# The third pair of feed-forward blocks by seven quarter products, and five lesser weight parts by adding transfers

## The chip, the cores and the metric

The kernel runs on one core of a Trainium2 chip. The metric is the time of one execution on the device in microseconds. The kernel before was timed in three runs: median 947.94 us, lowest 947.19, highest 948.01. The profile is of one more execution, which took 947.17 us, with a span of 945.5 us from its first to its last instruction.

The engines are named as in the profile: PE is TensorE's matmuls and PEld its weight loads, DVE is VectorE, ACT ScalarE, POOL GpSimd, SP SyncE. A trailing q (SPq, POOLq) is the engine's sequencer, which issues transfers.

## The reference

One layer of a streaming encoder block over 512 tokens of 1024 numbers, in float32. The change touches only its first step, a feed-forward block of 2816 hidden numbers:

```python
def _swiglu(x, w_in, w_out):
    gate, up = jnp.split(x @ w_in, 2, axis=-1)
    return (jax.nn.silu(gate) * up) @ w_out

h = h + 0.5 * _swiglu(_rmsnorm(h, ffn1_norm[i]), ffn1_w_in[i], ffn1_w_out[i])
```

Here `w_in` is 1024 x 5632 (2816 columns of gate, 2816 of up) and `w_out` 2816 x 1024. Behind it stand the mixer (convolution and gated linear attention), a second feed-forward block, a gated input embedding and a last norm; they stay as they are.

## The kernel before

**Two parts of every number.** Matmuls run on float32r. A float32 weight is split in a larger part `wh`, its rounding to float32r, and a lesser part `wl`, what the rounding left; activations likewise (`hgH` and `hgL`, `t2H` and `t2L`, `actH` and `actL`). A product is three matmuls (`mm3`, L209, and `mul`, L308): wh with the larger activation, wh with the lesser, wl with the larger. `high` (L183) makes wh with a cast on ACT. The lesser part is made in one of two ways. `low` (L193) subtracts wh from the raw weights on DVE. `added` (L198) writes the negated rounding of the raw weights to wl with a second pass on ACT; then a transfer issued from POOL adds the raw weights onto it in place:

```python
act.mul(l3, r3, -1.0)
pool.dma_start(out=l3.bitcast(F32), in_=r3, accum_op=ALU.add)
```

In the first feed-forward block every lesser part is made by `low`; `added` is used in the mixer, in the second feed-forward block and at the end.

**Pairs.** The 22 blocks of 128 hidden numbers are taken in 11 pairs (0 to 10; the third pair is pair 2). A pair's input weights are four tiles of 128 x 1024 numbers (512 KB): a11, a12 (gate columns, first and second half of the 1024 inputs), a21, a22 (up columns). Activations are held turned, hidden numbers in partitions, tokens in columns. Pair 0 is computed in the opening, while x arrives.

A *plain* pair takes eight units h0 to h7 (`plain_unit`, L694), each 12 matmuls 512 columns wide. Any other pair is computed as a 2 x 2 matrix of blocks times a 2 x 2 matrix (two halves of the inputs by two halves of the tokens) with seven quarter products in place of eight: units m1, m2, m6, m7, m5, m4, m3 (L659 to L692), each 24 matmuls 256 wide. These need four sums of weight tiles, s1 = a21 + a22, s2 = s1 - a11, s3 = a11 - a21, s4 = a12 - s2 (`s12`, `s3_`, `s4_`, on DVE; s3 and s4 overwrite the raw tiles a21 and a12), each split in two parts, and sums of activations t1 to t4 (class `Right`, L329), which are made once and used by all such pairs. t4 overwrites the tiles of a part of the plain activations, so it is made after the last plain unit.

In the kernel before, pairs 1 and 2 are plain (`plain` is `(1, 2)`) and pairs 3 to 10 take seven products.

**Output blocks.** When the hidden numbers of a stretch of `CUTS` are finished (pairs 0 and 1 for the first), four output units follow; each multiplies one w_out tile of 512 KB and yields two blocks of the output, 12 matmuls 512 wide for each. They are put between the units of the pairs behind.

**Order.** `ffn` (L604) lists the units; `drive` (L584) walks through them. A unit names what it needs and how many units ahead: the load of a raw tile 7 or 9 units, the sums 6, the two parts of a tile `AHEAD` = 4 (5 for s1). The jobs due ahead of a unit are issued first, then the first gating job left by the unit before, then the unit's matmuls and its hook, then what else was left (`act_parts` splits the gated product in actH and actL). PE, DVE and ACT each execute their instructions strictly in this program order (class `Ordered`); POOL's and SP's instructions are ordered by the scheduler. So a job on ACT or DVE that is not ready holds all behind it on that engine.

Hooks hang other work on units: `first_out` with pair 0's gating on h0 of pair 1; the pieces and row sums for `Right` on h1, h2, h3 of pair 1 (tiles xg); and the splitting of t2, t3, t1, t4 on the units named at L869.

**Buffers.** Raw weight tiles have six (`raw`), wh and wl six each, weight sums two, PSUM banks for matmuls seven. The raw buffer of a tile comes free when its last reader is done: `low` on DVE, a sum, or with `added` the transfer. A load on SP's queue waits for its buffer and holds the loads behind it.

Of the kernel before, what the change touches and what calls it, by code (L numbers as in the profile page):

```python
# [62 lines left out]
def block_kernel(ctx: ExitStack, tc: tile.TileContext, a: dict, out: bass.AP):  # L63
# [29 lines left out]
    def tmp(s, w=SEQ, dt=F32, bufs=2):  # L93
        return tp.tile([P, w], dt, tag=s, bufs=bufs, name=nm(s))

    def bank():
        return pp.tile([P, SEQ], F32, tag="mm", bufs=7, name=nm("ps"))

    def aux():
        return pp.tile([P, SEQ], F32, tag="aux", bufs=1, name=nm("ax"))  # L100
# [158 lines left out]
    def spread(col, copy=True):  # L259

        ps = aux()
        for j in range(TB):
            pe.transpose(ps[:, j * P:(j + 1) * P], col[:, j:j + 1].to_broadcast([P, P]), ident)
        if not copy:
            return ps
        bc = tmp("bc", bufs=1)
        act.copy(bc, ps)
        return bc
# [255 lines left out]
    ps0 = [bank() for _ in range(4)]  # L524
    split_w(0, 1, dve.tensor_copy)
    split_x(0)
    mid = []
# [22 lines left out]
    xb = Right(hg, "ffn1_norm")  # L550
# [31 lines left out]
    AHEAD = 4  # L582
# [18 lines left out]
        for f in left:  # L601
            f()

    def ffn(w_in, w_out, x, gname, given, first, rsb, hooks, plain):  # L604


        norm = Norm()
# [86 lines left out]
        def plain_unit(j):  # L694

            up, i, k = j // 4, j // 2 % 2, j % 2
            def run(p):
                if not j:
                    p.g, p.s = {}, {}
                if not k:  # L700
                    p.x = bank()
                ps = p.x
                wh, wl = p.part(f"a{1 + up}{1 + k}")
                cs = slice(i * P, (i + 1) * P)
                for c in range(4):
                    mm3(ps, wh[:, c, cs], wl[:, c, cs], *x.rows[4 * k + c], k == c == 0, k == 1 and c == 3)
                if not k:
                    return []
                if not up:
                    def gate():  # L710
                        p.s[i] = silu(scaled(ps, "g1"))
                    return [gate]
                return [lambda: gated_block(p, p.s[i], scaled(ps, "u1"), i),
                        lambda: act_parts(p) if i else None]
            return run
# [4 lines left out]
        def unit(kind, i):  # L720
            p = pairs[i]

            def go(run):
                left = run(p)
                hooks.get((kind, i), lambda *_: None)()
                return left

            if kind[0] == "h":
                j = int(kind[1])
                part, run = (f"a{1 + j // 4}{1 + j % 2}", plain_unit(j)) if j % 4 < 2 else (None, plain_unit(j))  # L730
                if part:
                    return [(AHEAD, lambda: p.part(part)), (9, lambda: p.fetch(part))], lambda: go(run)
            else:
                part, run = USES[kind]
            before = [(AHEAD + (kind == 'm5'), lambda: p.part(part))] if part else []
            if kind in ("m1", "m2"):
                before.append((7, lambda: p.fetch(part)))
            elif kind == "m6":
                before += [(9, lambda: p.fetch("a21", "a22")), (6, p.s12)]
            elif kind in ("m7", "m3"):  # L740
                before.append((6, p.s3_ if kind == "m7" else p.s4_))

            return before, lambda: go(run)
# [63 lines left out]
        def add(kind, i):  # L807
            if 0 <= i < npair and (kind, i) not in had:
                had.add((kind, i))
                units.append(unit(kind, i))  # L810
# [48 lines left out]
    w_in = a["w_in"][0]  # L859
    w_ahead = []  # L860

    def sums_hooks(x, names, at):

        h = {}
        for name, key in zip(names, at):
            h[key] = lambda *_, name=name: x.split(name)
        return h

    hooks = sums_hooks(xb, ("t2", "t3", "t1", "t4"), (("h5", 1), ("h7", 1), ("h3", 2), ("m1", 3)))  # L869
    hooks.update({("h%d" % (i + 1), 1): f for i, f in enumerate(steps[2:])})  # L870
    hooks.update({("m5", 3): lambda *_: made[0](), ("m5", 4): lambda *_: constants(),
                  ("m4", 10): lambda *_: w_ahead.append(ahead(w_in, D_CONV, 2 * P)),
                  ("last", 4): lambda *_: w_ahead.append(ahead(w_in, 0, 2 * P))})
    hg, norm = ffn(ffn1_in, a["ffn1_w_out"][0], xb, "mix_norm", {0: Left(ffn1_in, 0), 1: w1},
                   (ps0[:2], ps0[2:]), lambda: spread(mid[0]), hooks, (1, 2))
    pool.on = False
    cw, gwu, mean, mask, nbias = made

# [61 lines left out]
    mid = []  # L940
# [10 lines left out]
    rs, rsb = mid  # L951
# [471 lines left out]
    mid = []  # L1423
    xb = Right(hg, "ffn2_norm")
# [15 lines left out]
    hooks = sums_hooks(xb, ("t2", "t3", "t1", "t4"), (("h0", 1), ("h1", 1), ("h3", 1), ("m1", 2)))  # L1440
# [3 lines left out]
    q11, q21, q12, q22, b11, b21, t2, wproj = ([] for _ in range(8))  # L1444
# [59 lines left out]
    def todo(*fs):  # L1504
# [6 lines left out]
                  ("rest", 4): todo((q_high, b21, q21, 1), (first_sum, 1), (third_sum, 1)),  # L1511
                  ("rest", 6): todo((final_in,), (row_sums, 0))})
    hg, norm = ffn(ffn2_in, a["ffn2_w_out"][0], xb, "ple_norm", wf, ((g0, u0), (g1_, u1_)), mid[1], hooks, (1,))


# [144 lines left out]
    def kept(ps, name, **kw):  # L1660
        o = tmp(name, **kw)
        act.copy(o, ps)
        return o
# [20 lines left out]
    t1, t3 = q11, q12  # L1684
    n2_ = [x for jp in range(2) for x in split_rows(n2, jp)]
    project(0)
    m1 = [kept(p_, "sq", bufs=3) for p_ in x_]
# [98 lines left out]
```

## Time and profile before

| | |
|---|---|
| median of three runs | 947.94 us |
| the profiled execution | 947.17 us |
| its span | 945.5 us |
| ACT busy | 471.6 us (50%) |
| POOL busy | 56.4 us (6%) |
| mean granted TensorE clock | 0.997 of full speed |
| DMA, mean over the span | 119 GB/s |

A timeline row gives the start and the length in us, the engine, the line of the code (all operations that go through the helper `Ordered` have its line, 46), the operation and its tiles (written from read). The length of one matmul holds its way through the array, which overlaps the next one's; what counts on a busy PE is the distance of two starts. In square brackets stands how long the engine had been idle and what ended it. A row for a stretch (A:B) gives its length, then for each engine the busy time and the number of instructions, then the clock, the DMA engines' busy share and GB/s. A row for transfers gives the tiles, the queue, the count, the size and, where the trace has it, the time from issue to landing.

### The profile page before, as it was taken

The page shows a single profiled execution, that of the slowest core. Times are in us where ns is not written, and L with a number is a line of the kernel's source. Part 1 is how long each engine was busy: PE and PEld are TensorE (multiplying, and loading weights), DVE is VectorE, ACT ScalarE, POOL GpSimd, SP SyncE. Part 2 cuts the span into 40 slices and gives each one's busy share as a digit, 9 for nine tenths or more (in the row PEclk, how much of TensorE's full clock was granted, in tenths as well). Part 3 has the DMA queues.
Part 4 walks back from the last instruction along what each step waited for, and adds up shares of the span by engine and source line. Part 5 has one row for each costly group of instructions (what it writes and reads, how often), then busy time and mean ns, then how long its engine had stood idle before and what let it go on. Part 6 is the DMA issues. An engine that isn't in the chain of part 4 may idle for free.

```text
span 945.5 us, 14381 instructions
## 1 busy us (share of the span) xinstructions
PE 934.8 (99%) x5770; PEld 828.2 (88%) x5770; DVE 747.0 (79%) x1021; ACT 471.6 (50%) x713; POOL 56.4 (6%) x71
## 2 busy tenths in 40 slices
PE   9999999999999999999999999999999999999996
PEld 7888999999999988788877889999999999998885
DVE  6786887887788566999986749787878787866896
ACT  5752544334443574463564855444434433445882
POOL 0000200000000110001030010000000000000121
PEclk9999999999999999999999999999999999999998
DMA  7532223242223593346552571432243224347463
GB/s 229 182 123 74 94 79 119 94 134 89 91 89 112 146 254 84 77 109 161 134 132 74 151 178 45 134 110 70 89 134 112 68 91 132 97 149 222 90 111 112
DMA packets 107686, 112.88 MB, mean 119 GB/s; under 512 B 5139, under 2 KB 96453, under 8 KB 107620
## 3 DMA queue, kind: packets, MB, share of 16 engines
q1 hardware_dynamic: 101732, 94.67, 31.9%
q0 software_dynamic: 5872, 17.30, 10.3%
q8 instruction: 45, 0.74, 0.3%
q14 instruction: 21, 0.17, 0.1%
q10 hardware_dynamic: 16, 0.00, 0.0%
HBM read 93.61 MB, written 2.10 MB: 101 GB/s over the span
## 4 chain that ended last, share of the span: by engine, by line
PE 99%; DVE 0%; ACT 0%; POOLq 0%; issue 0%; POOL 0%
PE ps L46 97%; PE ax L46 1%; DVE y L46 0%; POOLq L1782 0%; ACT ycH L46 0%; DVE yc L46 0%; ACT hgH L46 0%; DVE rs L46 0%; ACT s L46 0%; DVE u L46 0%; DVE g L46 0%; DVE s L46 0%; POOL ident masks.py:199 0%; DVE ms L46 0%; POOL mean L46 0%
## 5 line engine op out<-in xcount | busy, mean ns | idle before, releaser
L46 PE MATMUL ps<-hgH,wh 128*128 128x256 f32 (+1 forms) x768 | 238.4, 315 | 0.3 <-ACT hgH L46 0.3
L46 PE MATMUL ps<-hgL,wh 128*128 128x256 f32 (+1 forms) x768 | 237.6, 314 | 0.0
L46 PE MATMUL ps<-hgH,wl 128*128 128x256 f32 (+1 forms) x768 | 237.3, 314 | 0.0
L46 DVE TENSOR_TENSOR wl<-wr,wh 128x1024 fp32r<-128x1024 f32 (+2 forms) x162 | 189.6, 1181 | 47.8 <-ACT wh L46 47.7
L46 ACT CAST wh<-wr 128x1024 fp32r<-128x1024 f32 (+2 forms) x176 | 176.7, 1019 | 30.8 <-PE ps L46 16.3
L46 PEld LDWEIGHTS ps<-hgH,wh 128*128 128x128 f32 x768 | 146.3, 191 | 11.2 <-issue 1.1
L46 PEld LDWEIGHTS ps<-hgL,wh 128*128 128x128 f32 x768 | 146.1, 191 | 9.2 <-issue 0.2
L46 PEld LDWEIGHTS ps<-hgH,wl 128*128 128x128 f32 x768 | 146.4, 191 | 8.8
L46 PE MATMUL ps<-actH,wh 128*128 128x512 f32 x352 | 137.4, 390 | 0.0
L46 PE MATMUL ps<-actL,wh 128*128 128x512 f32 x352 | 137.3, 390 | 0.0
L46 PE MATMUL ps<-actH,wl 128*128 128x512 f32 x352 | 136.9, 389 | 0.0
L46 ACT ACTIVATE s<-g 128x512 f32<-128x512 f32 x48 | 30.4, 633 | 194.3 <-DVE g L46 194.3
L46 DVE SCALAR_TENSOR_TENSOR cv<-glu,cw,cv 128x502 f32<-128x502 f32 (+24 forms) x120 | 81.0, 732 | 0.6
L46 PEld LDWEIGHTS ps<-actH,wl 128*128 128x128 f32 x352 | 66.1, 188 | 14.1
L46 PEld LDWEIGHTS ps<-actH,wh 128*128 128x128 f32 x352 | 66.2, 188 | 12.9
L46 PEld LDWEIGHTS ps<-actL,wh 128*128 128x128 f32 x352 | 66.2, 188 | 12.5
L46 DVE SCALAR_TENSOR_TENSOR h<-ps,h 128x512 f32<-128x512 f32 x80 | 54.1, 687 | 22.2 <-PE ps L46 22.0
L46 ACT COPY sq<-ps 128x512 f32<-128x512 f32 x38 | 22.1, 585 | 73.8 <-PE ps L46 73.8
L46 DVE TENSOR_TENSOR wl<-sm,wh 128x1024 fp32r<-128x1024 f32 x38 | 46.2, 1221 | 1.2 <-ACT wh L46 0.9
L46 ACT CAST actH<-m 128x512 fp32r<-128x512 f32 x44 | 25.5, 618 | 37.3 <-DVE m L46 37.2
L46 ACT CAST wh<-sm 128x1024 fp32r<-128x1024 f32 x38 | 39.5, 1043 | 5.5 <-DVE sm L46 2.9
L46 DVE TENSOR_TENSOR u<-ps,sq 128x512 f32<-128x512 f32 x17 | 11.7, 691 | 34.8 <-ACT sq L46 34.8
(267 smaller groups left out, 1729.5 us busy)
## 6 DMA issues: line engine op xcount, KB each, us to landing
wr<-in_ffn_w_in SPq DMA_DIRECT2D x84, 512.0 KB
wr<-in_ffn_w_out SPq DMA_DIRECT2D x32, 512.0 KB
wr<-in_w_in SPq DMA_DIRECT2D x20, 512.0 KB
wl<-wr POOLq DMA_DIRECT2D x15, 512.0 KB, 5.5
wr<-in_ffn_w_out SPq DMA_DIRECT2D x16, 384.0 KB
wr<-in_w_out SPq DMA_DIRECT2D x8, 512.0 KB
wq<-in_ple_w_gate SPq DMA_DIRECT2D x8, 512.0 KB
wl<-wq POOLq DMA_DIRECT2D x8, 512.0 KB, 5.1
```

Source lines behind the costliest of these rows:

```text
L46: inst = call(*args, **kwargs)
```

## The change

The first feed-forward block has one plain pair fewer: `plain` is `(1,)`, so pair 2 takes seven products. Since they need t1 to t4 earlier, t2, t3 and t1 are now split on h4, h5 and h6 of pair 1 and t4 on m1 of pair 2. Five lesser parts are made by `added` in place of `low`: those of a21 and a22 of pair 1 (units h4 and h5; still four units ahead) and of a11, a12 and a22 of pair 2 (units m1, m2 and m4; six units ahead). The second feed-forward block passes no `adds` and stays as it is.

```diff
-    def ffn(w_in, w_out, x, gname, given, first, rsb, hooks, plain):
+    def ffn(w_in, w_out, x, gname, given, first, rsb, hooks, plain, adds=()):
...
                 part, run = (f"a{1 + j // 4}{1 + j % 2}", plain_unit(j)) if j % 4 < 2 else (None, plain_unit(j))
                 if part:
-                    return [(AHEAD, lambda: p.part(part)), (9, lambda: p.fetch(part))], lambda: go(run)
+                    make = p.add_part if (kind, i) in adds else p.part
+                    return [(AHEAD, lambda: make(part)), (9, lambda: p.fetch(part))], lambda: go(run)
             else:
                 part, run = USES[kind]
-            before = [(AHEAD + (kind == 'm5'), lambda: p.part(part))] if part else []
+            if (kind, i) in adds:
+                before = [(AHEAD + 2, lambda: p.add_part(part))]
+            else:
+                before = [(AHEAD + (kind == 'm5'), lambda: p.part(part))] if part else []
...
-    hooks = sums_hooks(xb, ("t2", "t3", "t1", "t4"), (("h5", 1), ("h7", 1), ("h3", 2), ("m1", 3)))
+    hooks = sums_hooks(xb, ("t2", "t3", "t1", "t4"), (("h4", 1), ("h5", 1), ("h6", 1), ("m1", 2)))
...
-                   (ps0[:2], ps0[2:]), lambda: spread(mid[0]), hooks, (1, 2))
+                   (ps0[:2], ps0[2:]), lambda: spread(mid[0]), hooks, (1,),
+                   {("h4", 1), ("h5", 1), ("m1", 2), ("m2", 2), ("m4", 2)})
```

`add_part`, which the kernel already has for the second feed-forward block (L412):

```python
def add_part(self, *names):
    for name in names:
        self.done[name] = added(high(getattr(self, name)))[:2]
```

The order of the units from the second pair on, where o is an output unit of the first stretch:

```
before  h0 .. h7 (pair 1)  h0 h1 h2 o h3 o h4 h5 o h6 h7 o (pair 2)  m1.3 m2.3 m1.4 m6.3 ...
after   h0 .. h7 (pair 1)  m1.2 m2.2 m1.3 m6.2 m7.2 m5.2 m2.3 o m4.2 m3.2 o m6.3 m7.3 m5.3 m1.4 m2.4 o ...
```

## The prediction

> **What bounds the kernel now.** I read the head of the profile's page first, then the chain of waits in order of time, then the timelines of the engines over the stretch that changes (31 to 131 us).
>
> ```profile
> span 945.5 us, 14381 instructions
> PE 934.8 (99%) x5770; PEld 828.2 (88%) x5770; DVE 747.0 (79%) x1021; ACT 471.6 (50%) x713; POOL 56.4 (6%) x71
> ```
> ```profile
> 34.69 79.86 PE ps L46 x420
> ```
>
> TensorE is busy 99% of the span, and the second row, a piece of the chain of waits (start, length, what), says that it ran 420 matmuls in one piece from 34.69 to 114.55 us. That piece holds the whole second and third pair. So nothing there waits for another engine today: the change can win only matmul time, and any wait it makes is lost in full. VectorE, at 79%, is next. The run profiled took 947.17 us, 1.67 more than its span; the median of the three timed runs is 947.94, 0.77 above it. 0.2% is 1.9 us, about what a measurement of this kernel tells from no change.
>
> **TensorE: eight units out, seven in.** A plain unit (h) is 12 matmuls 512 wide, a product unit (m) 24 matmuls 256 wide. Rows of the timeline (start, us, engine):
>
> ```profile
> 42.72 0.39 PE L46 MATMUL ps<-hgH,wh 128*128 128x512 f32 x1
> ...
> 45.44 0.39 PE L46 MATMUL ps<-hgH,wh 128*128 128x512 f32 x1
> 45.66 0.39 PE L46 MATMUL ps<-hgL,wh 128*128 128x512 f32 x1
> 45.89 0.39 PE L46 MATMUL ps<-hgH,wl 128*128 128x512 f32 x1
> ```
> ```profile
> 97.11 0.28 PE L46 MATMUL ps<-hgH,wh 128*128 128x256 f32 x1
> ...
> 105.75 0.28 PE L46 MATMUL ps<-t2H,wh 128*128 128x256 f32 x1
> ```
>
> From 42.72 (start of h4 of pair 1) to 45.44 (start of h5) are 12 starts: 2.72 us a unit, 0.2267 a matmul. From 97.11 (m1 of pair 3) to 105.75 (m6) are 72 starts: 0.1200 each, 2.88 a unit. Half the width costs more than half the time, so removing 8 x 2.72 = 21.76 and adding 7 x 2.88 = 20.16 leaves **-1.60 us**, not an eighth of the pair. That is 0.17%, and no other work on the path is removed: it is the whole possible gain.
>
> **The second pair's lesser weights, on the path.** For a22 of pair 1, low (VectorE) becomes added: a second ScalarE pass, then a transfer from POOL's queue that adds the weights onto it. Its due place doesn't move: still four units ahead of h5. The rows of today:
>
> ```profile
> 33.02 1.04 ACT L46 CAST wh<-wr 128x1024 fp32r<-128x1024 f32 x1
> 34.72 0.59 ACT L46 COPY bc<-ax 128x512 f32<-128x512 f32 x1 [0.66 <-PE ax L46]
> ...
> 40.01 0.62 ACT L46 CAST actH<-m 128x512 fp32r<-128x512 f32 x1 [0.25 <-DVE m L46]
> 40.54 1.05 ACT L46 CAST wh<-wr 128x1024 fp32r<-128x1024 f32 x1
> 41.49 1.70 ACT L46 ACTIVATE xg<-h,vcol 128x256 f32<-128x256 f32 x4
> ```
> ```profile
> 41.62 1.23 DVE L46 TENSOR_TENSOR wl<-wr,wh 128x1024 fp32r<-128x1024 f32 x1 [0.26 <-ACT wh L46]
> ```
>
> The cast at 40.54 is a22's, behind pair 0's two actH casts, and its lesser part is finished at 42.85, 3.0 us before h5 reads it as wl (45.89, above). What an adding transfer costs shows later in the same trace:
>
> ```profile
> 373.09 1.03 ACT L46 CAST wh<-wr 128x1024 fp32r<-128x1024 f32 x1
> 374.03 1.06 ACT L46 ACTIVATE wl<-wr 128x1024 fp32r<-128x1024 f32 x1
> ```
> ```profile
> 375.38 0.92 POOL L46 DMA_DIRECT2D wl<-wr  x1 [9.47 <-ACT wl L46]
> ```
> ```profile
> wl<-wr POOLq DMA_DIRECT2D x1, 512.0 KB, 4.6
> ```
> ```profile
> DMA to landing us min/median/max: 4.5/5.5/8.4
> ```
>
> Cast to second pass 0.94, second pass 1.06, 0.29 until POOL starts, 4.6 us to landing for this one (fourth row). The last row is all 23 transfers of 512 KB that write a lesser part: never under 4.5. So for a22: a21's extra pass ends at 33.02 + 0.94 + 1.06 = 35.02 and holds the copy bc, which starts at 34.72 today, back by some 0.23; pair 0's gating chain hangs on it, so the cast starts at 40.77, the second pass at 41.71, POOL at 43.06, and the part **lands at 47.66. h5 wants it at 45.89: TensorE waits 1.8 us.** I take 4.6, not the median, because little else moves then:
>
> ```profile
> 41.00:44.00 3.00, 3.00 (x15) 2.49 (x14) 2.70 (x4) 2.19 (x5) 0.00 (x0) 1.00 0.02 5
> 44.00:48.00 4.00, 4.00 (x20) 3.30 (x19) 2.06 (x4) 2.10 (x5) 0.00 (x0) 1.00 0.42 135
> ```
>
> The DMA engines are 2% busy from 41 to 44 (the last two figures are their share and GB/s), and the load that fills 44 to 48 today starts about 3 us earlier in the new order, when a21's landing frees a raw buffer. Bounds: 4.5 gives 1.7 us, 8.4 gives 5.6.
>
> [...]
>
> **The other four transfers.** a21 (pass ends 35.02, POOL 35.3, landing 39.9) has until the third matmul of h4, 43.17; it would take 7.9 us to be late. The two of pair 2 follow on ScalarE between the xg pieces: 2.a11's pass ends at 46.2 and lands near 51.1, for m1 at 53.6; 2.a12's at 50.3, landing near 55.2, for m2 at 56.5. After the first wait both places are 1.8 later. 2.a22 has over 7 us. On POOL only the reciprocal root at 29.4 stands ahead; the mask's memsets wait for a buffer until 97 us today and stay behind. On SP's queue the raw buffers of added parts come free at a landing and not after low: 3.a11 about 40, 3.a12 about 48, each over 8 us before its cast.
>
> **VectorE and ScalarE between the wait and the first output unit.** Five lows go, but pair 2 now needs four sums, four lows of sums, and nine gating operations for six. These bring a second due date. The nearest rows:
>
> ```profile
> 48.16 2.14 DVE L46 TENSOR_TENSOR xg<-xg,xg 128x512 f32<-128x512 f32 x3 [2.06 <-ACT xg L46]
> ...
> 88.29 1.23 DVE L46 TENSOR_TENSOR sm<-sm,wr 128x1024 f32<-128x1024 f32 x1
> 89.44 1.22 DVE L46 TENSOR_TENSOR wl<-wr,wh 128x1024 fp32r<-128x1024 f32 x1
> ...
> 101.39 1.43 DVE L46 TENSOR_TENSOR hgL<-xg,hgH 128x256 fp32r<-128x256 f32 x4
> ```
> ```profile
> 35.34 0.69 DVE L46 TENSOR_TENSOR g<-ps,bc 128x512 f32<-128x512 f32 x1
> 35.95 0.68 DVE L46 TENSOR_TENSOR u<-ps,bc 128x512 f32<-128x512 f32 x1
> ```
> ```profile
> 48.20:73.60 25.40, 25.40 (x114) 21.03 (x113) 21.44 (x28) 12.92 (x19) 0.00 (x0) 1.00 0.45 140
> ```
>
> Back to back a 1024-wide operation takes 1.15 us, a 512-wide one 0.61, the four for t4 1.35. VectorE's last three row sums (48.16 today, about 48.4 after) start the count. From there to the lesser part of the first w_out tile, program order has 10 wide operations (four sums; lows of 3.a11, s2, s1, s3, 3.a12, w_out), 18 of 512 and t4: 11.5 + 11.0 + 1.35 = 23.8 us. It also has three waits for ScalarE: 1.3 for t2's casts, behind 2.a12's cast and pass; about 1.5 where pair 1's actH casts wait for VectorE and 2.a22's cast and pass and 3.a12's cast stand behind them (0.94 x 3 against 1.2 of actL); about 1.1 at the w_out cast, behind pair 2's silu and a copy. So the tile is ready near 48.4 + 27.7 = 76.1. Without any wait TensorE reads it at 53.6 (h7's end, 45.44 + 3 x 2.72) + 7 x 2.88 + 0.45 = 74.2: **1.9 us late**. If TensorE has already waited 1.8 at h5, only 0.1 is left: the two don't add up, the later one counts. The last row is today's load there: VectorE busy 21.44 of 25.40. Bounds for this step: without the three waits it ends at 72.2 and costs nothing; with each wait half as long again, 2.0 more. Earlier readers have slack after the wait at h5: s2's low about 1.5 us, s3's about 2. Behind it each pair has two output units of 24 x 0.2267 us again, as pairs 3 to 10 have today, and catches up.
>
> **Sum.** Against the profiled span: 945.5 - 1.60 + 1.95 (the later of the waits and a little at the restart) = 945.85, **+0.35 us**; on the median, 947.94 + 0.35 = **948.3 us**.
>
> **Rivals.** (1) *Both waits are hidden*: the transfer lands by 45.89, so 2.8 us after POOL starts, and VectorE's chain comes out 2 us shorter. 947.94 - 1.60 = 946.3. For it: today nothing waits there, and VectorE's idle time is spread over many gaps I may have counted too coarsely. Against it: no such transfer of 23 took under 4.5. [...] (2) *Slower: a22's transfer is slowed by loads*. Place: the third matmul of h5. It decides once the landing takes more than 6.3 us, since 43.06 + 6.3 - 45.89 - 1.60 = 1.9. The row for it, a transfer with a weight load issued beside it:
>
> ```profile
> wl<-wr POOLq DMA_DIRECT2D x1, 512.0 KB, 8.4
> wr<-in_w_out SPq DMA_DIRECT2D x1, 512.0 KB
> ```
>
> At 8.4 it is +4.0: 951.9; at 6.5, +2.1: 950.0. Against it: the quiet 41 to 44 above. (3) *The first output unit decides*: VectorE's chain comes 2.0 us later than worked out, 3.9 us of waiting, +2.3: 950.2. For it: ScalarE and VectorE wait for each other three times within 25 us; against it, the transfers take five lows off VectorE.
>
> **Chances.** Forecast (0 to +1.2 us, landings of 4.5 to 5.6) 0.60; (1) 0.10; (2) 0.16; (3) 0.14. Rival (1) gains 1.60, inside 0.2%, so faster by over 0.2% has only what a mis-sized saving leaves: 0.05. Slower by over 0.2%: most of (2), half of (3) and a tail of the forecast, 0.23. Within 0.2%: 0.72. The range goes from (1) to between (2)'s two prices: 946.2 to 950.9.
>
> **What would show it.** In the changed kernel's chain of waits the unbroken TensorE piece is cut at h5 of pair 1, near 46 to 48 us, by a wait for the adding transfer of about 1.8 us, and hardly again at the first output unit (actH matmuls near 76). A ps piece of 24 matmuls should still last 2.88 us. A cut of over 3 us at h5 shows rival (2); one at actH of over 1 us, rival (3); no cut, rival (1). The forecast is wrong if m units take another time than 2.88, if the transfer lands in less than 4 us, or if a wait stands at m1, m2 or m6 of pair 2.

## The result and the profile after

| | before | after |
|---|---|---|
| median of 5 runs each | 947.94 us | 956.08 us |
| lowest and highest | 947.19, 948.17 | 954.79, 957.38 |
| the profiled execution, its span | 947.17, 945.5 | 954.79, 953.0 |

The ratio is 1.0086, 95% interval 1.0075 to 1.0097: slower by 8.1 us, far outside the range of the prediction. One thing is needed to read single numbers: in five of the eleven profiles the opening takes about 2 us more. The four matmuls that spread pair 0's row factors (`ax<-ident,rs`) then start at 36.0 to 36.4 instead of 34.0 to 34.6; where a profile has the late opening, times below are therefore compared from that start. Both profiles of the table have the early one (before 34.09, after 33.97).

The head of the page after:

```profile
span 953.0 us, 14561 instructions
PE 936.7 (98%) x5842; PEld 832.7 (87%) x5842; DVE 751.6 (79%) x1026; ACT 481.5 (51%) x724; POOL 58.5 (6%) x76
```

TensorE has 72 matmuls more than before (168 of a product pair for 96 of a plain one) and 1.9 us more busy time, though the matmuls that were exchanged take 1.6 us less; this is the first sign that some of them ran slowly. The chain of waits (start, length, what) no longer has the piece of 420 matmuls. What stands in its place, in excerpts:

```profile
41.67 0.96 ACT wl L46
...
67.30 1.04 ACT wh L46
68.34 0.96 ACT wl L46
69.30 0.95 ACT wh L46
70.28 1.23 DVE wl L46
...
72.14 0.70 DVE g L46
...
74.81 0.59 ACT u L46
75.45 32.81 PE ps L46 x216
```

The chain that decides leaves TensorE at 24.66, runs for 51 us through ScalarE and VectorE, handed from one to the other again and again, and comes back to TensorE only at 75.45. Where TensorE stood, its timeline shows. First the third matmul of h5 of pair 1, the place that the prediction named:

```profile
45.55 0.39 PE L46 MATMUL ps<-hgL,wh 128*128 128x512 f32 x1
47.89 0.50 PE L46 MATMUL ps<-hgH,wl 128*128 128x512 f32 x1 [1.96 <-DMA wl<-wr]
...
49.39 0.61 PE L46 MATMUL ps<-hgH,wl 128*128 128x512 f32 x1
49.79 0.63 PE L46 MATMUL ps<-hgH,wh 128*128 128x512 f32 x1
...
52.78 0.41 PE L46 MATMUL ps<-hgL,wh 128*128 128x512 f32 x1
```

The two starts 45.55 and 47.89 should be 0.23 apart and are 2.34 apart: 2.11 us lost to the adding transfer. And then something that the prediction did not have: from 49.39 to 52.78 there are 8 starts, 0.424 apart instead of 0.2267. That costs 3.39 - 8 x 0.2267 = 1.58 us more. The second place is m5 of pair 2:

```profile
71.64 0.28 PE L46 MATMUL ps<-t3H,wl 128*128 128x256 f32 x1
75.45 0.39 PE L46 MATMUL ps<-t1H,wh 128*128 128x256 f32 x1 [3.53 <-ACT u L46]
...
76.75 0.41 PE L46 MATMUL ps<-t1L,wh 128*128 128x256 f32 x1
...
80.15 0.28 PE L46 MATMUL ps<-hgH,wl 128*128 128x256 f32 x1
```

3.81 between two starts instead of 0.12, so 3.69 us lost, and again a slow stretch: 16 starts from 76.75 to 80.15, 1.48 us more than at 0.12. The rows by stretches have the granted clock third from the end:

```profile
50.00:53.00 3.00, 3.00 (x8) 2.32 (x8) 1.73 (x4) 2.02 (x5) 0.86 (x1) 0.53 1.03 243
...
78.00:80.00 2.00, 2.00 (x12) 2.00 (x11) 1.97 (x2) 0.02 (x1) 0.00 (x0) 0.50 0.60 203
```

About half clock behind each wait; before had 1.00 throughout this part. The sum: -1.60 (the exchange) + 2.11 + 1.58 + 3.69 + 1.48 + 0.2 (a slower first step behind each wait) = +7.5, which is the growth of the span, 953.0 - 945.5.

Why m5 waits is read from ScalarE's timeline:

```profile
66.77 0.62 ACT L46 CAST actH<-m 128x512 fp32r<-128x512 f32 x1 [3.99 <-DVE m L46]
67.30 1.04 ACT L46 CAST wh<-wr 128x1024 fp32r<-128x1024 f32 x1
68.25 1.05 ACT L46 ACTIVATE wl<-wr 128x1024 fp32r<-128x1024 f32 x1
69.21 1.04 ACT L46 CAST wh<-wr 128x1024 fp32r<-128x1024 f32 x1
72.86 0.63 ACT L46 ACTIVATE s<-g 128x512 f32<-128x512 f32 x1 [2.62 <-DVE g L46]
73.40 0.57 ACT L46 COPY sq<-ps 128x512 f32<-128x512 f32 x1
73.86 1.05 ACT L46 CAST wh<-wr 128x1024 fp32r<-128x1024 f32 x1
74.81 0.59 ACT L46 COPY u<-ps 128x512 f32<-128x512 f32 x1
```

m1, m6 and m5 of a pair add onto one PSUM bank. Between m6 and m5 its content has to be copied out (`u2 = snap(p.x)` in `m6`), and the copy is an instruction of ScalarE. m6's matmuls are done near 68.9, yet the copy `u<-ps` runs at 74.81: it stands behind the whole row above it. ScalarE itself waited 3.99 us for pair 1's gated product, then had two casts and a pass, then waited 2.62 us for VectorE's sums of m2. No operand of m5 was late (VectorE's last one for it, s1's lesser part, was finished at 64.27); the bank was.

### The profile page after: what moved, and what is told of

Same layout as the page of the kernel before. It is cut to its first block, busy times and chain, and to the rows that moved or that the text cites. A ratio compares the mean times of both kernels' runs of the same rounds, so it can differ in the third digit from the quotient of the medians.

```text
span 953.0 us, 14561 instructions
## 1 busy us (share of the span) xinstructions
PE 936.7 (98%) x5842; PEld 832.7 (87%) x5842; DVE 751.6 (79%) x1026; ACT 481.5 (51%) x724; POOL 58.5 (6%) x76
## 4 chain that ended last, share of the span: by engine, by line
PE 93%; ACT 3%; DVE 2%; issue 1%; POOLq 0%; POOL 0%; DVEq 0%; ACTq 0%
PE ps L46 92%; PE ax L46 1%; ACT wh L46 1%; ACT xg L46 1%; DVE wl L46 1%; ACT wl L46 0%; DVE g L46 0%; ACT s L46 0%; DVE m L46 0%; DVE xg L46 0%; ACT hgH L46 0%; DVE u L46 0%; ACT sq L46 0%; DVE y L46 0%; DVE t1L L46 0%
## 5 line engine op out<-in xcount | busy, mean ns | idle before, releaser
L46 PE MATMUL ps<-hgH,wl 128*128 128x256 f32 (+1 forms) x768 | 234.7, 311 | 2.0 <-DMA wl<-wr 2.0
L46 PE MATMUL ps<-hgH,wh 128*128 128x256 f32 (+1 forms) x768 | 235.8, 312 | 0.4 <-ACT hgH L46 0.4
L46 PE MATMUL ps<-hgL,wh 128*128 128x256 f32 (+1 forms) x768 | 234.9, 311 | 0.0
L46 DVE TENSOR_TENSOR wl<-wr,wh 128x1024 fp32r<-128x1024 f32 (+2 forms) x158 | 185.0, 1181 | 46.6 <-ACT wh L46 46.5
L46 DVE TENSOR_TENSOR wl<-sm,wh 128x1024 fp32r<-128x1024 f32 x40 | 48.5, 1221 | 0.8 <-ACT wh L46 0.4
L46 PE MATMUL ps<-t1H,wh 128*128 128x256 f32 x144 | 41.5, 288 | 3.5 <-ACT u L46 3.5
L46 ACT CAST wh<-sm 128x1024 fp32r<-128x1024 f32 x40 | 41.7, 1046 | 3.1 <-DMA sm<-in_ple_w_gate 1.0
```

Source lines behind the costliest of these rows:

```text
L46: inst = call(*args, **kwargs)
```

## The experiments

Ratios are to the kernel before, timed beside each run (its medians were 947.81, 947.89 and 947.78). First, parts of the change alone.

**Pair 1's two adding transfers alone** (pair 2 stays plain, hooks as before):

```diff
-    hooks = sums_hooks(xb, ("t2", "t3", "t1", "t4"), (("h4", 1), ("h5", 1), ("h6", 1), ("m1", 2)))
+    hooks = sums_hooks(xb, ("t2", "t3", "t1", "t4"), (("h5", 1), ("h7", 1), ("h3", 2), ("m1", 3)))
...
-                   (ps0[:2], ps0[2:]), lambda: spread(mid[0]), hooks, (1,),
-                   {("h4", 1), ("h5", 1), ("m1", 2), ("m2", 2), ("m4", 2)})
+                   (ps0[:2], ps0[2:]), lambda: spread(mid[0]), hooks, (1, 2),
+                   {("h4", 1), ("h5", 1)})
```

> Pair 2 stays plain; only the lesser parts of a21 and a22 of pair 1 are made by adding transfers. Theory (wait plus half clock): the wait at h5 of pair 1, 2.1 us, is the transfer's alone, and the matmuls behind it run for about 3.4 us at half the clock, 1.6 us more: 947.9 + 3.7 = 951.6. Rival (the slow matmuls come with the products or with the denser transfers of the change, not with the wait): the wait alone, 950.0. Rival of the prediction as written (a wait costs its own length): 1.8 us, 949.7.

Measured 953.12 (951.41 to 953.38, 4 runs), ratio 1.0053 (1.0038 to 1.0068). The wait and the slow stretch, in its timeline:

```profile
50.28 0.50 PE L46 MATMUL ps<-hgH,wl 128*128 128x512 f32 x1 [1.93 <-DMA wl<-wr]
...
51.77 0.62 PE L46 MATMUL ps<-hgH,wl 128*128 128x512 f32 x1
...
55.17 0.40 PE L46 MATMUL ps<-hgL,wh 128*128 128x512 f32 x1
```

The place and the wait are those of after, without any product in the pair, and again 8 starts at half clock (3.40 us, 0.425 apart; the granted clock from 53 to 56 us, which the slow stretch fills in part, was 0.64). The profiled run, 953.38, has the late opening (its spread starts at 36.39, 2.30 behind before). From the same start its span is 951.6 - 2.3 = 949.3, 3.8 above before's 945.5, where the theory said 3.7; only the lowest run has the time that it gave.

**Pair 1 by subtraction, the three transfers of pair 2 kept:**

```diff
-                   {("h4", 1), ("h5", 1), ("m1", 2), ("m2", 2), ("m4", 2)})
+                   {("m1", 2), ("m2", 2), ("m4", 2)})
```

> The change, with the lesser parts of pair 1 by VectorE again. Theory (one backlog, two due dates): TensorE is not cut at h5, so it reaches m5 of pair 2 some 3.7 us earlier while ScalarE and VectorE come no sooner; the wait there grows from 3.7 to about 5.7 us, with some 1.5 us of half clock behind it: 947.9 - 1.6 + 5.7 + 1.5 = 953.5. Rival (two independent waits): the 2.1 + 1.6 us at h5 go and m5 keeps its 3.7: 956.1 - 3.7 = 952.4 and a wait of 3.7 at m5.

Measured 956.66 (955.53 to 957.6, 4 runs), ratio 1.0093 (1.0078 to 1.0108): no better than after, though the wait at h5 is gone.

```profile
77.24 0.58 PE L46 MATMUL ps<-t1H,wh 128*128 128x256 f32 x1 [6.47 <-ACT u L46]
...
82.31 0.32 PE L46 MATMUL ps<-t1H,wl 128*128 128x256 f32 x1
```

This profile has the late opening (36.33, 2.36 behind after). From the same start, m5 begins at 77.24 - 2.36 = 74.9, hardly earlier than after's 75.45: the chain through VectorE and ScalarE sets it, and TensorE, 3.8 us ahead because nothing held it at h5, waits there instead. The half clock lasted longer (5.07 us from the restart, its starts 0.214 apart, the granted clock 0.50 from 76 to 82 us), which takes back the 0.5. So the waits did not add up, as theory said; its 953.5 was too low by the longer half clock and by a wait of 6.47 where it had 5.7.

**No adding transfer at all** (the set of adds empty):

> The changed kernel with none of the five adding transfers: pair 2 by seven products, every lesser part by subtraction on VectorE. Theory (VectorE's work between pair 1 and the first output unit is what is late, and the transfers only relieve it): the wait at h5 is gone, and the one at the fifth product of pair 2 (m5), 3.5 us with five transfers and 6.5 with three, stays at 5 us or more with half clock behind it, and new waits of about 0.5 us appear ahead of it; -1.6 + 5 to 7 + about 3 of half clock = 955 to 957. Rival (the transfers themselves, by their pass on ScalarE or their landing, make the waits): without them only -1.6 and the bank copy's own time are left, 946.3 to 949.

Measured 956.4 (956.04 to 957.32, 4 runs), ratio 1.0089 (1.0076 to 1.0102), as theory said; the rival's 946 to 949 falls. Pair 2's waits now start earlier (two more, of 0.34 and 0.53 us, stand between these rows):

```profile
58.41 0.39 PE L46 MATMUL ps<-hgH,wl 128*128 128x256 f32 x1 [1.33 <-DVE wl L46]
...
76.74 0.58 PE L46 MATMUL ps<-t1H,wh 128*128 128x256 f32 x1 [5.41 <-ACT u L46]
```

With five transfers, three or none, the medians lie within a microsecond. From the same start of the spread, the profiled spans are 953.0, 955.6 - 2.36 = 953.2 and 955.0 - 0.34 = 954.7, so the kernel without transfers is the slowest of the three. The transfers are not what makes the change slow.

**m5 of pair 2 in a bank of its own**, so that it does not wait for the copy. This kernel leaves out the sum of m1 and m6 of pair 2 from what m5 and m3 add to:

```diff
         def m5(p):
+            fresh = plain == (1,) and p is pairs[2] and adds
+            if fresh:
+                p.x = bank()
-            mul(p.x, p.part("s1"), x.op["t1"], False, False)
+            mul(p.x, p.part("s1"), x.op["t1"], bool(fresh), False)
```

> The change, with m5 of pair 2 starting a bank of its own, so that it leaves out the sum of m1 and m6 and need not wait until ScalarE has copied that bank. Theory (m5 waits for the copy alone): the 3.7 us at m5 and the half clock behind it, 1.5 us, go; the next readers of late work (the w_out tile at the first output unit, ready near 76.2) come after it: 956.1 - 5.2 = 950.9, with the wait at h5 left. Rival (m5 waits for s1 or t1 as well, or the wait moves on to the first output unit): less than 2 us gained, 954 or more, and a cut at m5 or at the first actH matmul.

Measured 950.23 (949.93 to 952.0, 9 runs), ratio 1.0028 (1.0019 to 1.0038): 5.9 us less than after, so the wait for the copy is the cause of most of the loss.

```profile
48.45 0.50 PE L46 MATMUL ps<-hgH,wl 128*128 128x512 f32 x1 [1.93 <-DMA wl<-wr]
...
82.57 0.39 PE L46 MATMUL ps<-hgH,wh 128*128 128x256 f32 x1 [0.45 <-DVE u L46]
...
100.74 0.38 PE L46 MATMUL ps<-t1H,wh 128*128 128x256 f32 x1 [0.95 <-ACT u L46]
```

At the first output unit, where the prediction saw the late chain arrive, there is no wait. But m4 of pair 2 waits 0.45 us until VectorE has read the bank that m7 filled, and m5 of pair 3 waits 0.95 us for its own bank's copy. The wait at h5 had no slow stretch behind it in this profile (starts 0.23 apart throughout). From the same start of the spread (34.56 here) the gain is 5.0 us: about 5.3 at m5 and behind it and 1.6 behind h5, less 1.7 at the two new waits.

**The same with pair 1 by subtraction** (both edits above):

> Both of the above: pair 1's lesser parts by VectorE, and m5 of pair 2 in a bank of its own (the sum of m1 and m6 left out there). Theory: no wait of over 1.5 us is left in the stretch, so the saved matmul time shows: between 946.3 (nothing waits) and 948.2 (two small waits, 0.3 at the first output unit and up to 1.4 at m5 of pair 3, no half clock). Rival (the products bring a loss of their own, by denser transfers or slower matmuls): 950 or more without a long wait in the trace.

Measured 949.87 (949.44 to 952.15, 9 runs), ratio 1.0025 (1.0015 to 1.0035): above the 946.3 to 948.2 expected. Nothing waits at h5, and the time it saves reappears in four small waits:

```profile
74.92 0.50 PE L46 MATMUL ps<-actH,wh 128*128 128x512 f32 x1 [0.23 <-ACT wh L46]
76.18 0.50 PE L46 MATMUL ps<-actH,wl 128*128 128x512 f32 x1 [0.52 <-DVE wl L46]
81.96 0.39 PE L46 MATMUL ps<-hgH,wh 128*128 128x256 f32 x1 [0.49 <-DVE u L46]
100.15 0.39 PE L46 MATMUL ps<-t1H,wh 128*128 128x256 f32 x1 [0.96 <-ACT u L46]
```

The first two are the output unit of the prediction, which TensorE now reaches early enough to find its tile late; the others are the two banks again. With the restarts the four cost 2.9 us. It is one backlog, and whichever reader comes first pays for it.

**Is the half clock TensorE's idleness?** Matmuls that nobody reads fill the two waits:

```diff
+        def fill(n, w, xh):
+            idle = aux()
+            for _ in range(n):
+                pe.matmul(idle, w, xh, start=True, stop=True)
...
         def m5(p):
+            if p is pairs[2] and adds:
+                fill(22, p.part("s1")[0][:, 0, 0:P], x.rows[0][0])
...
                 for c in range(4):
+                    if j == 5 and c == 0 and adds:
+                        fill(8, wh[:, c, cs], x.rows[4][0])
```

> The changed kernel with matmuls that nobody reads put into its two waits: 8 of 512 columns ahead of the first matmul of h5 of pair 1 (1.8 us at full clock) and 22 ahead of m5 of pair 2 (5.0 us). Theory (TensorE's idle time brings the half clock behind each wait; m5's start is set by VectorE and ScalarE at a fixed time, near 75.4 us, so what h5 saves is lost again in the wait at m5): no half clock behind either place, 1.4 to 1.6 us less: 954.5, from 953.8 to 955.2. Rival (the half clock comes with the load on the chip or from run to run, not with idle time): the filling matmuls or those behind them run at 0.427 us a start, and the time is 956 or above. Second rival (the half clock at h5 delays VectorE's work too): 953 or less.

Measured 954.26 (953.99 to 955.51, 5 runs), ratio 1.0066 (1.0053 to 1.0079): 954.5 was expected. In its profile (late opening, the spread at 36.18, 2.21 behind after):

```profile
50.43 0.50 PE L46 MATMUL ps<-hgH,wl 128*128 128x512 f32 x1 [0.48 <-DMA wl<-wr]
...
72.67 5.18 PE L46 MATMUL ax<-hgH,wh 128*128 128x512 f32 x22
77.68 0.32 PE L46 MATMUL ps<-t1H,wh 128*128 128x256 f32 x1
```

The 22 take 0.228 each, and no row from 48 to 90 us is at half clock (granted 1.00 in each): with TensorE kept busy in the same places of the same work, the slow stretches are gone. The copy that m5 waits for, on ScalarE:

```profile
76.97 0.58 ACT L46 COPY u<-ps 128x512 f32<-128x512 f32 x1
```

76.97 - 2.21 = 74.76, and after has it at 74.81, although TensorE now reached m5's place 1.3 us sooner (72.67 - 2.21 = 70.46 against 71.76). So of the two slow stretches only the second cost time: what the first took, the wait at m5 was shorter by.

**Is there too much work for VectorE and ScalarE here, or is it badly placed?** Three other orders of nearly the same work, with another choice of the parts that go by transfer. The first has six transfers, for the first two tiles of pairs 2, 3 and 4 and none in pair 1, splits t2, t3, t1 and t4 one to two units later, and lets the parts due ahead of each unit be set one by one:

```diff
...
-                before = [(AHEAD + 2, lambda: p.add_part(part))]
+                before = [(far.get((kind, i), AHEAD + 2), lambda: p.add_part(part))]
...
-                before = [(AHEAD + (kind == 'm5'), lambda: p.part(part))] if part else []
+                before = [(far.get((kind, i), AHEAD + (kind == 'm5')), lambda: p.part(part))] if part else []
...
-                return [(7, get), (AHEAD, make)], run
+                return [(7, get), (far.get((f0, n), AHEAD), make)], run
...
-    hooks = sums_hooks(xb, ("t2", "t3", "t1", "t4"), (("h4", 1), ("h5", 1), ("h6", 1), ("m1", 2)))
+    hooks = sums_hooks(xb, ("t2", "t3", "t1", "t4"), (("h5", 1), ("h6", 1), ("m1", 2), ("m2", 2)))
...
-                   {("h4", 1), ("h5", 1), ("m1", 2), ("m2", 2), ("m4", 2)})
+                   {("m1", 2), ("m2", 2), ("m1", 3), ("m2", 3), ("m1", 4), ("m2", 4)},
+                   {("m4", 2): 3, ("m5", 2): 5, ("m6", 2): 4, ("m7", 2): 4, ("m2", 3): 5, ("m1", 3): 3,
+                    ("m5", 3): 4, ("m6", 3): 4, ("m7", 3): 4, (0, 0): 3, (0, 2): 3})
```

> Seven products for pair 2 with another order of the same work: pair 1 by subtraction; transfers for the first two tiles of pairs 2, 3 and 4 instead; t2, t3, t1, t4 split one to two units later; and the parts due three to five units ahead instead of four to six where their reader allows it. Adding up the rows of the changed kernel's timeline in this order leaves one wait of about 0.9 us (at m1 of pair 3, its transfer). Theory (order and due places made the waits, the engines have room): 947.9 - 1.6 + 0.9 + 0.4 for the spread's place = 947.6, from 946.5 to 949, no half clock. Rival (VectorE and ScalarE have too much to do in these 30 us whatever the order): waits of 3 us and more in sum as in the run with its own bank, 949.5 or above.

The second differs from it in these lines:

```diff
-    hooks = sums_hooks(xb, ("t2", "t3", "t1", "t4"), (("h5", 1), ("h6", 1), ("m1", 2), ("m2", 2)))
+    hooks = sums_hooks(xb, ("t2", "t3", "t1", "t4"), (("h5", 1), ("h6", 1), ("m1", 2), ("m7", 2)))
...
-                   {("m1", 2), ("m2", 2), ("m1", 3), ("m2", 3), ("m1", 4), ("m2", 4)},
-                   {("m4", 2): 3, ("m5", 2): 5, ("m6", 2): 4, ("m7", 2): 4, ("m2", 3): 5, ("m1", 3): 3,
-                    ("m5", 3): 4, ("m6", 3): 4, ("m7", 3): 4, (0, 0): 3, (0, 2): 3})
+                   {("h4", 1), ("m1", 2), ("m2", 2), ("m1", 3), ("m2", 3), ("m4", 3), ("m2", 4)},
+                   {("m4", 2): 2, ("m5", 2): 4, ("m6", 2): 4, ("m7", 2): 3, ("m2", 3): 4, ("m1", 3): 4,
+                    ("m5", 3): 5, ("m6", 3): 3, ("m7", 3): 4, (0, 0): 4, (0, 2): 3})
```

> A second order of the same work: one transfer in pair 1 (a21), the first two tiles of pair 2, the first two and the last of pair 3 and the second of pair 4; t4 split at m7 of pair 2; the part for m4 of pair 2 due two units ahead. The same addition leaves waits of 1.4 us in sum. Theory: 947.9 - 1.6 + 1.4 + 0.4 = 948.1, from 947 to 949.5. Rival (too much work whatever the order): 949.5 or above.

The first: 949.02 (947.79 to 951.38, 12 runs), ratio 1.0008 (0.9999 to 1.0018), just above the 949 that theory allowed. The second: 950.56 (950.06 to 952.38, 8 runs), ratio 1.003 (1.002 to 1.0039), a miss: its waits came to 3.5 us and not 1.4, and the time is the rival's. The two longest are m4 of pair 2, whose part is due only two units ahead, and the bank copy of m5 of pair 3:

```profile
82.41 0.39 PE L46 MATMUL ps<-hgH,wl 128*128 128x256 f32 x1 [1.41 <-DVE wl L46]
...
100.79 0.39 PE L46 MATMUL ps<-t1H,wh 128*128 128x256 f32 x1 [1.40 <-ACT u L46]
```

The first kernel's profile has one wait, longer than worked out, and half clock behind it (granted 0.59 from 64 to 68 us):

```profile
63.56 0.39 PE L46 MATMUL ps<-hgH,wl 128*128 128x256 f32 x1 [1.76 <-DMA wl<-wr]
...
64.73 0.40 PE L46 MATMUL ps<-hgH,wl 128*128 128x256 f32 x1
...
68.13 0.29 PE L46 MATMUL ps<-t2H,wh 128*128 128x256 f32 x1
```

It is m1 of pair 3, and its transfer was issued a unit too late. The third order mends only that:

```diff
-                   {("m4", 2): 3, ("m5", 2): 5, ("m6", 2): 4, ("m7", 2): 4, ("m2", 3): 5, ("m1", 3): 3,
+                   {("m4", 2): 3, ("m5", 2): 5, ("m6", 2): 4, ("m7", 2): 4, ("m2", 3): 4, ("m1", 3): 4,
```

> The order of the run e6_order_a, with the transfers for the first two tiles of pair 3 both due four units ahead (three and five there). In the profile of that run its one wait, 1.76 us, stood at the first product of pair 3, whose transfer started on POOL 58.6 us into the span, one unit too late, and half clock followed it. Theory: with the transfer a unit earlier that wait is gone, the same addition of rows leaves 0.4 us at m5 of pair 2 and no half clock: 947.9 - 1.6 + 0.4 + 0.4 for the spread's place = 947.1, from 946.3 to 948.3. Rival (VectorE and ScalarE hold too much work here, so the wait only moves on to m5 or m2 of pair 3): 1.5 us of waits or more, 948.5 or above.

Measured 947.6 (947.27 to 949.42, 11 runs), ratio 0.9997 (0.9988 to 1.0006): the time of before. What is left in the profile:

```profile
62.11 0.38 PE L46 MATMUL ps<-hgH,wl 128*128 128x256 f32 x1 [0.43 <-DMA wl<-wr]
...
71.30 0.39 PE L46 MATMUL ps<-t1H,wh 128*128 128x256 f32 x1 [0.54 <-ACT u L46]
```

By the distances of the starts, these two with their restarts cost 1.5 us, and there is no half clock (granted 1.00 in every row from 30 to 110 us). The spread starts at 36.02, 1.93 behind before; from the same start the span is 947.5 - 1.93 = 945.6, before's 945.5, so the two waits take up the 1.6 us that the products save. But the engines do have room for the work: the 8 us came from its order and from which parts went by transfer. m5, no longer held for 3.5 us, still waits for the same copy, which in its profile stands ahead of the w_out cast and not behind it:

```profile
70.19 0.57 ACT L46 COPY sq<-ps 128x512 f32<-128x512 f32 x1
70.66 0.59 ACT L46 COPY u<-ps 128x512 f32<-128x512 f32 x1
```

No run separates the order from the choice of the transfers. Between its last row sums and m2's gate, VectorE makes three lesser parts in this run and five in after, because the first two tiles of pair 3 go by transfer; at 1.15 us each that is about 2.3 us of the 6.2 by which the copy comes sooner (it ends at 71.25 - 2.05 = 69.2, with the spread 2.05 behind after, and not at 75.4).

## Why the prediction was wrong, step by step

**TensorE, -1.60 us:** right. m6 and m7 of pair 2, from after's timeline:

```profile
66.00 0.28 PE L46 MATMUL ps<-t2H,wh 128*128 128x256 f32 x1
...
68.88 0.28 PE L46 MATMUL ps<-t3H,wh 128*128 128x256 f32 x1
```

2.88 us a unit, as predicted, and the third order's account closes with it to 0.2 us.

**a22 of pair 1, 1.8 us at the third matmul of h5:** right in place, cause and nearly in size (2.11). POOL took the transfer at 42.94 (43.06 predicted). Rival (2), the slowed transfer, did not happen; the five of the change, from issue to landing:

```profile
DMA to landing us min/median/max: 4.5/4.9/6.5
```

But the half clock behind the wait was missing; "a little at the restart", 0.05 us of the 1.95, was 1.7 here. Both proved to cost nothing in the end: without the wait and what followed it, the change is as slow.

**The other four transfers have time:** right; none of their readers waits.

**VectorE's chain to the first w_out tile, ready near 76.1:** right in its order, its operations and its three waits, and to 0.1 us, which is partly luck: the waits came to 3.25 us (1.27, 1.00, 0.98) for 3.9, the operations with the gaps between them to 24.6 for 23.8. The tile's subtraction in after:

```profile
74.94 1.23 DVE L46 TENSOR_TENSOR wl<-wr,wh 128x1024 fp32r<-128x1024 f32 x1 [0.98 <-ACT wh L46]
```

**The step that failed:** "Earlier readers have slack after the wait at h5: s2's low about 1.5 us, s3's about 2." I went only through the readers of weight parts. m5 adds onto the bank that m6 filled, and waits for the copy of it, which in ScalarE's order stands directly behind the very w_out cast whose lateness I had just worked out (about 1.1 us of waiting "at the w_out cast, behind pair 2's silu and a copy"; the copy that I counted is that of m1 of pair 3, and m6's comes next behind the cast). By the prediction's own numbers TensorE wants that bank at 53.6 + 5 x 2.88 = 68.0 if nothing waits; the copy ended at 75.4. That is 7.4 us late, not 1.9, and it is the whole result: -1.6 + 7.4 + 1.5 of half clock behind it = +7.3, where the prediction put nothing at m5 and 0.05 at a restart. "The two don't add up, the later one counts" was right as a rule, and the run without pair 1's transfers confirmed it; applied to the wrong reader it gave 0.1.

**"Behind it each pair ... catches up":** true of after itself, where TensorE does not stop again up to 108 us, but only because it comes so late. With m5 of pair 2 in its own bank, m5 of pair 3 waited 0.95 us at 100.74.

**The rivals:** none of the three had this place. Rival (3) had the right cause (VectorE and ScalarE waiting for each other) with the wrong reader. The prediction's own test, "a wait stands at m1, m2 or m6 of pair 2", did not list m5 either.

## What to carry to other kernels

A matmul waits not only for its operands but for the bank that it adds onto (m5 of pair 2 for 3.53 us): where a sum in PSUM is copied out between two products, put the copy into the list of readers, with its place in the copying engine's queue. When an engine with strict order falls behind, ask for every instruction behind the late one who waits for it, and when that reader would have run had nothing waited. Six of the seven waits of 1.76 to 6.47 us in these runs were followed by half clock, which cost another 1.5 to 2.3 us each; and before giving up a change that saves matmul time, try another order of what prepares it, since here the order and the choice of the transfers together were worth 8 us.

## What the runs showed of the hardware that was not expected

Half clock after short waits. Behind waits of 1.76, 1.93, 1.96 and 3.53 us TensorE ran at full clock for another 1.2 to 1.5 us, and then for 3.4 us at half (64.73 to 68.13, 51.77 to 55.17, 49.39 to 52.78, 76.75 to 80.15; the granted clock in the last of them, from 78 to 80, was 0.50). Behind the waits of 5.41 and 6.47 us it was slow from its first matmul on, for some 5.1 us (77.24 to 82.31 in the latter; granted 0.50 from 76 to 80 in both). With the waits filled there was none, nor behind the waits of up to 1.41 us (granted 1.00). But the 1.93 us in the run with m5's own bank brought none either (granted 1.00 from 48 to 56), while 1.93 us did with pair 1's transfers alone: the length of a wait does not decide alone. What else decides was not shown.
